# Where three blocks of attention and their output projection are woven into the rest of a hybrid attention and mLSTM layer

## The chip, the cores and the metric

One core of a Trainium2 chip runs the whole program. The metric is the device time of one execution in microseconds, the median of several runs. The engines are TensorE (PE, with its weight loads as PEld), VectorE (DVE), ScalarE (ACT), GpSimd (POOL), and SyncE (SP), whose queue issues nearly all DMAs.

## What is computed

One layer on 1152 tokens in 9 blocks of 128: block 0 is a prompt, blocks 1 to 8 are latent tokens of one request. Attention (8 query heads of 64, 2 key heads) and a bidirectional mLSTM (4 heads of 128) read one input projection, and one output projection merges them; a SwiGLU FFN of width 2816 follows. Cut to what matters:

```python
h = rmsnorm(x, norm1_w) * (1 + sc1) + sh1
aq, ak, av, mq, mk, mv, mo, mg = jnp.split(h @ w_in, SPLIT_POINTS, axis=-1)
attn_o = attention(rope(rmsnorm(aq)), keys, vals)   # prompt: own keys; latent: 1024 + 128 context keys
hm, st_f, st_b = mlstm_bidir(mq, mk, mv, gates, init_f, init_b)
hm = rmsnorm(hm, mlstm_norm_w) * sigmoid(mo)
x = x + g1 * (jnp.concatenate([attn_o, hm], axis=-1) @ w_out)
h2 = rmsnorm(x, norm2_w) * (1 + sc2) + sh2
x = x + g2 * ((silu(h2 @ w_g) * (h2 @ w_u)) @ w_down)
y = rmsnorm(x, final_norm_w)
```

All is float32; the kernel splits operands into a high and a low part and takes three products for one.

## The kernel before

The 9 blocks are treated in three groups of three (CB = 3; group c has blocks 3c to 3c + 2). The program is one long order of instructions. Work that should run side by side is written as Python generators, each `yield` a unit, and `weave(main, side, n_main, n_side)` steps `side` n_side times over n_main units of `main`, evenly. `beside` steps several generators, each at its rate; `chain` puts generators one behind another. A scheduler then orders each engine's instructions by a priority, which is the place in the program, and by when it reckons their inputs to be ready; `hot(n)` moves a block n places ahead, and `tc.issue_after(x)` has instructions on x's engine issue behind x. Each engine then runs its own order strictly.

The stages, in the order of the program:

1. Modulations, the key, value and query projections.
2. The four mLSTM heads: for each, `head_project` (its part of w_in, 96 units), woven with the scan of the head before (`head_mlstm`) and with `att`, the attention.
3. The last head's scan, with the attention's half of the output projection of group 0 (`attn_out_first`).
4. `prefill`: the mLSTM half of the output projection of all blocks, and norm2 of group 0. It steps `att` by 0.35 of a unit each of its 33 steps.
5. The FFN of group 0 (`groups`, five groups of FFN columns in GROUPS). Beside the first three (`GROUPS[:NG]`, 192 units after the first four steps) runs `attention_side`: some scales, what is left of `att`, the attention's half of the output projection of group 1, the attention of group 2, twenty empty units and the output projection of group 2. Then the attention's pools in SBUF are closed (`es_att.close()`), others open in their place, and beside the last two groups (180 units) run the features of groups 1 and 2 (`features6`).
6. The FFN of groups 1 and 2 together, with seven products in the place of eight (`pair6`, `down6`), and the end (`down_last`).

The attention of a group is the generator `attention(c, oT, done, ha, hv, spill)`. For each block it loads q (tile `qr`), transposes it on PE into a PSUM bank of tag `mm`, and copies it as a high and a low part to `qT`, of which there is one. Then for each of 8 heads: S (six products, L1128) into the one tile `S`; its maximum on DVE (L1130); exp on ACT (L1131); the scaled high part on ACT (L1134) and low part on DVE (L1135); and their transposes as DMAs of SP (L1137, L1138). After each pair of heads the values (L1152, L1153) are multiplied, one pair late. Where `spill` is given, the output of a block (`oS`) goes to DRAM (`o_d`), else it stays in three tiles `oT`. Blocks other than 0 have 1152 keys; block 0 has 128.

`attn_out` is the output projection of one group: it takes a place `home(i)` for each block's high and low part, loads a block's o from DRAM if it was spilled, loads w_out in four pieces (`out_pieces`), multiplies (L1250 to L1254) and adds to x1. A weight piece (`load_piece`) is a DMA into one of two `raw` buffers, a cast on ACT (L174) and a difference on DVE (L145). Where the o was not spilled the pieces issue behind the last transpose:

```python
with nullcontext() if spilled else tc.issue_after(loaded["turned"]):
    ws = out_pieces(0, n)
```

The working PSUM banks at that stage are four of tag `mm` (a gate and up pair takes two, a down product up to two at once, transposes one) beside three for S and one, `po`, for the values.

Of the kernel before, what the change touches and what calls it, by code (L numbers as in the profile page):

```python
# [8 lines left out]
F32 = mybir.dt.float32  # L9
F32R = mybir.dt.float32r  # L10
# [9 lines left out]
P = 128  # L20
# [5 lines left out]
NQ = 8  # L26
# [7 lines left out]
CB = 3  # L34
NCH = NB // CB
CT = CB * P
GROUPS = [(0, 4), (4, 4), (8, 4), (12, 5), (17, 5)]
# [5 lines left out]
NG = 3  # L43
# [6 lines left out]
def hybrid_step(ctx: ExitStack, tc: tile.TileContext, I: dict, O: dict):  # L50
# [11 lines left out]
    def nm(s):  # L62
        uid[0] += 1
        return f"{s}_{uid[0]}"

    def weave(main, side, n_main, n_side):

        due = 0.0
        for units in main:
            due += n_side / n_main * (units or 1)  # L70
            while due >= 1.0:
                next(side, None)
                due -= 1.0
# [5 lines left out]
    def chain(*gens):  # L79
        for g in gens:  # L80
            for v in g:
                yield v
# [20 lines left out]
    drp = ctx.enter_context(tc.tile_pool(name="drp", bufs=1, space=DRAM, reuse_waits="tile"))  # L103
# [10 lines left out]
    q_d = [drp.tile([P, 512], F32, name=f"q_d{b}") for b in range(NB)]  # L114
    hm_d = [drp.tile([P, NH, CT] if c else [CT, 512], F32, name=f"hm_d{c}") for c in range(NCH)]
    g_d = drp.tile([2, 2, D], F32, name="g_d")
    o_d = [drp.tile([P, 512], F32, name=f"o_d{i}") for i in range(CB)]
    x1_d = [drp.tile([P, D], F32, name=f"x1_d{i}") for i in range(CB)]

    ident = cp.tile([P, P], F32, name="ident")  # L120
# [868 lines left out]
    def beside(*sides):  # L989

        due = [0.0] * len(sides)
        while True:
            for i, (g, rate) in enumerate(sides):
                due[i] += rate
                while due[i] >= 1.0:
                    next(g, None)
                    due[i] -= 1.0
            yield
# [24 lines left out]
    mix_spare = [t[:, 2 * (NB + 1) * P :].rearrange("p (k x) -> p k x", k=4) for t in big]  # L1023
# [34 lines left out]
    sts = [{} for _ in range(NH)]  # L1058
# [20 lines left out]
    ap = es_att.enter_context(tc.tile_pool(name="ap", bufs=1, side="right", reuse_waits="tile"))  # L1079
    ap2 = es_att.enter_context(tc.tile_pool(name="ap2", bufs=1, side="right", reuse_waits="tile"))  # L1080
# [95 lines left out]
    def new_x1(c):  # L1176
        if c == 1:
            x1 = x1p.tile([P, CB, D], F32, name=nm("x1"))
            return [x1[:, i, :] for i in range(CB)]
        x1 = [xe.tile([P, D], F32, name=nm("x1"), tag="mx", bufs=3) for _ in range(CB)]  # L1180
        for i in range(CB):
            dma(x1[i], x1_d[i])
        return x1
# [54 lines left out]
    def row_pair(row):  # L1238
        gs = []
        for n in range(2):  # L1240
            gl = xe.tile([P, 512], F32, name=nm("hmr"), tag="hmr", bufs=2)
            dma(gl, row[n * 512 : (n + 1) * 512].rearrange("(o n) -> o n", o=1).to_broadcast([P, 512]))
            gs.append(gl)
        return gs
# [160 lines left out]
    def attn_out(a, oT, row, home, spilled=None):  # L1405

        gs = row_pair(row)
        x1, parts = a["x1"], []
        for i in range(CB):
            th, tl = home(i)  # L1410
            parts.append((th, tl))
            o = oT[i]
            if spilled:
                o = t2().rearrange("p (k x) -> p k x", k=4)
                dma(o, spilled[i].rearrange("p (k x) -> p k x", k=4))
            with hot(500):
                nc.scalar.copy(th, o)
                sub(tl, o, th.bitcast(F32), "dve")
        for n in range(2):
            with nullcontext() if spilled else tc.issue_after(loaded["turned"]):  # L1420
                ws = out_pieces(0, n)
            for i, (th, tl) in enumerate(parts):
                ps = out_block([ws], 0, th, tl)
                with hot(200):
                    add_gated(x1[i], ps, gs[n], n)
                yield
        with hot(200):
            a["rs"] = stats(x1)
        yield
# [96 lines left out]
    def six_scales():  # L1526

        dve.tensor_reduce(out=six[:, 6:7], in_=shift2[:, :, 1], axis=AX.X, op=ALU.max, apply_absolute_value=True)
        dve.tensor_reduce(out=six[:, 7:8], in_=scale2[:, :, 1], axis=AX.X, op=ALU.max, apply_absolute_value=True)
        dve.scalar_tensor_tensor(out=six[:, 7:8], in0=six[:, 7:8], scalar=float(D) ** 0.5, in1=six[:, 6:7], op0=ALU.mult, op1=ALU.add)  # L1530
        yield
        yield from power_scale(fp, ones, six[:, 7:8], six[:, 0:2])
        for t, src in ((0, scale2), (1, shift2)):
            dve.tensor_scalar(out=mods6[:, :, t], in0=src[:, :, 1], scalar1=six[:, 0:1], scalar2=None, op0=ALU.mult)
        yield
# [201 lines left out]
    done = set()  # L1737
    o1 = []
    att0 = attention(0, oT, done, 200, 100)
    att = chain(att0, attention(1, o1, set(), 200, 100, o_d))  # L1740
    weave(head_project(0, sts[0]), beside((att, 0.16),), 96, 96)
    for h in range(1, NH):
        scan = head_mlstm(h - 1, sts[h - 1])
        sts[h]["scan"] = head_mlstm(h, sts[h])
        weave(head_project(h, sts[h]), beside((scan, 0.42), (att, 0.17)), 96, 96)
        emit(scan)
    scan = sts[NH - 1]["scan"]
    first, ada, x1_first, ahead = attn_out_first(oT, done)
# [12 lines left out]
    xe = ctx.enter_context(tc.tile_pool(name="xe", bufs=1, reuse_waits="tile"))  # L1761
# [18 lines left out]
    cur, nxt = {}, {}  # L1780
# [16 lines left out]

    far = {}

    def mixing(i):  # L1800
        if i == 1:
            return mix_spare
        if i == 2:
            t = ap2.tile([P, 3 * CT], F32R, name=nm("mx"), tag="pr", bufs=2)[:, 0:1024].rearrange("p (q n) -> p q n", q=NQ)
        else:
            t = ap.tile([P, NQ, P], F32R, name=nm("mx"), tag="qT", bufs=1)
        return t[:, 0:4], t[:, 4:8]

    def mixing_mx(i):
        t = xe.tile([P, NQ, P], F32R, name=nm("mx"), tag="mx", bufs=3)  # L1810
        return t[:, 0:4], t[:, 4:8]

    def attention_side():
        yield from six_scales()
        yield from att
        yield from attn_out(nxt, o1, g_d[0, 1], mixing_mx, o_d)
        far["x1"] = new_x1(2)
        o2 = []
        yield from attention(2, o2, set())
        for _ in range(20):  # L1820
            yield
        yield from attn_out(far, o2, g_d[0, 1], mixing)

    main = groups(0, cur, GROUPS[:NG])
    with tc.issue_after(loaded["gate"]):
        for _ in range(4):
            next(main)
    side = attention_side()
    weave(main, side, 18 * sum(nf for _, nf in GROUPS[:NG]) - 24, 80)
    emit(side)  # L1830
    es_att.close()
    es_6 = ExitStack()
# [1 line left out]
    a4p = es_6.enter_context(tc.tile_pool(name="a4p", bufs=1, side="right", reuse_waits="tile"))  # L1834
    sp = es_6.enter_context(tc.tile_pool(name="sp", bufs=1, side="right", reuse_waits="tile"))
    Bt = btp.tile([P, 7, 2, 4, CT], F16, name="Bt")
    firsts = []
    feats = chain(*[features6(nxt, 1, i, Bt, firsts) for i in range(CB)], *[features6(far, 2, i, Bt, firsts) for i in range(CB)])
    main = groups(0, cur, GROUPS[NG:])
    weave(main, feats, 18 * sum(nf for _, nf in GROUPS[NG:]), 40)  # L1840
    emit(feats)
    weight_scale()
    es_f.close()
# [80 lines left out]
```

## Time and profile before

| | us |
|---|---|
| median of 3 runs | 1562.74 |
| lowest, highest | 1561.05, 1563.01 |
| profiled execution | 1565.84 |
| its span, first to last instruction | 1564.1 |

| engine | busy us | share |
|---|---|---|
| PE | 1443.9 | 92% |
| PE weight loads | 1071.6 | 69% |
| DVE | 1130.5 | 72% |
| ACT | 811.9 | 52% |
| POOL | 216.3 | 14% |

The mean granted clock of TensorE was 0.963. Times in the trace are microseconds from the span's start. L12 is line 12 of the kernel. A row of the timeline has start, length, engine, line, operation, output and inputs, number of instructions merged, and in brackets the idle time of the engine before it and what ended that. SPq and ACTq are DMA issues. Matmuls are pipelined, so a product lasts longer than the distance to the next, and a busy PE is not for that alone a full one.

### The profile page before, as it was taken

How to read it: one execution, taken by the hardware profiler on the slowest of the kernel's cores; microseconds unless marked ns; L12 is line 12 of the kernel's file. 1: busy time of each engine (PE TensorE's matmuls, PEld its weight loads, DVE VectorE, ACT ScalarE, POOL GpSimd, SP SyncE). 2: the span in 40 equal slices, each digit the busy share in tenths (PEclk: the TensorE clock that was granted, in tenths of full speed). 3: DMA queues.
4: the chain of work that ended last, by engine and by line, in shares of the span. 5: the costliest groups of instructions: out<-in, count | busy, mean ns of one | idle time of the engine just before them, and what ended most of it. 6: DMA issues, size and time to landing. Idle time of an engine off the chain costs nothing. (4 is left out here: it accounts for less than half of the span.)

```text
span 1564.1 us, 22771 instructions
## 1 busy us (share of the span) xinstructions
PE 1443.9 (92%) x8281; PEld 1071.6 (69%) x8281; DVE 1130.5 (72%) x2272; ACT 811.9 (52%) x1524; POOL 216.3 (14%) x310
## 2 busy tenths in 40 slices
PE   6889899998998899998897779989999999999994
PEld 3635567776776678888796579975666767676763
DVE  4978557676768685677776566859879596886856
ACT  4855477867666454637575366735425151523233
POOL 0121323233234243000000001010000000000000
PEclk9999999999999999999898789999999999999997
DMA  9575226563558548658585533444313030312112
GB/s 368 150 232 174 66 74 95 112 106 67 99 146 212 175 113 197 195 168 201 124 179 98 153 114 117 146 143 146 96 41 121 19 121 23 122 61 74 35 35 81
DMA packets 254454, 195.45 MB, mean 125 GB/s; under 512 B 167878, under 2 KB 209046, under 8 KB 254342
## 3 DMA queue, kind: packets, MB, share of 16 engines
q1 hardware_dynamic: 251774, 189.56, 44.9%
q10 hardware_dynamic: 2440, 4.05, 0.7%
q8 instruction: 65, 1.06, 0.3%
q14 instruction: 47, 0.39, 0.1%
q0 software_dynamic: 128, 0.39, 0.1%
HBM read 143.15 MB, written 12.47 MB: 100 GB/s over the span
## 5 line engine op out<-in xcount | busy, mean ns | idle before, releaser
L1619 PE MATMUL mm<-Bt,A 128*128 128x384 f16 x616 | 200.6, 328 | 3.4 <-ACT A L1605 3.4
L1620 PE MATMUL mm<-Bt,A 128*128 128x384 f16 x616 | 202.0, 328 | 0.0
L1621 PE MATMUL mm<-Bt,A 128*128 128x384 f16 x616 | 197.8, 327 | 0.0
L174 ACT CAST whi<-raw 128x1024 fp32r<-128x1024 f32 (+1 forms) x102 | 103.1, 1013 | 130.9 <-DMA raw<-in_w_down_dram 58.2
L145 DVE TENSOR_TENSOR wlo<-raw,whi 128x1024 fp32r<-128x1024 f32 (+1 forms) x102 | 122.5, 1203 | 54.5 <-ACT whi L174 52.3
L1135 DVE SCALAR_TENSOR_TENSOR pl<-pr,st,ph 128x1152 f16<-128x1152 f32 (+1 forms) x72 | 95.9, 1333 | 41.1 <-ACT ph L1134 39.6
L1472 PE MATMUL mm<-aTh,whi 128*128 128x384 f32 x352 | 120.7, 343 | 0.7 <-ACT whi L174 0.4
L1474 PE MATMUL mm<-aTh,wlo 128*128 128x384 f32 x352 | 120.2, 342 | 0.8 <-DVE wlo L145 0.8
L1131 ACT ACTIVATE pr<-S,st 128x1152 f32<-128x1152 f32 (+1 forms) x72 | 81.3, 1129 | 75.9 <-DVE st L1130 70.9
L1473 PE MATMUL mm<-aTl,whi 128*128 128x384 f32 x352 | 119.9, 341 | 0.0
L1128 PE MATMUL S<-kst,qT 128*128 128x384 f32 (+1 forms) x400 | 92.2, 364 | 21.7 <-ACT pr L1131 21.6
L1130 DVE TENSOR_REDUCE st<-S 128x1 f32<-128x1152 f32 (+1 forms) x72 | 88.9, 1235 | 22.5 <-PE S L1128 21.1
L525 PE MATMUL wi<-headw,hT 128*128 128x384 f16 x288 | 94.6, 328 | 0.6 <-ACT th L815 0.6
L527 PE MATMUL wi<-headw,hT 128*128 128x384 f16 x288 | 94.5, 328 | 0.0
L526 PE MATMUL wi<-headw,hT 128*128 128x384 f16 x288 | 94.5, 328 | 0.0
L1134 ACT ACTIVATE ph<-pr,st 128x1152 f16<-128x1152 f32 (+1 forms) x72 | 83.8, 1163 | 18.7 <-ACT pr L1131 5.6
L1619 PEld LDWEIGHTS <-A 128*128 128x128 f16 x616 | 60.5, 98 | 47.0 <-ACT A L1605 4.2
L1128 PEld LDWEIGHTS S<-kst,qT 128*128 128x128 f32 x400 | 73.0, 198 | 28.0 <-ACT pr L1131 25.4
L1605 ACT ACTIVATE A<-S,six 128x1024 f16<-128x1024 f32 x44 | 50.2, 1147 | 73.5 <-PE mm L1621 59.5
L1621 PEld LDWEIGHTS <-A 128*128 128x128 f16 x616 | 60.5, 98 | 40.4 <-issue 0.5
L1620 PEld LDWEIGHTS <-A 128*128 128x128 f16 x616 | 60.6, 98 | 39.5 <-issue 0.9
L1203 DVE TENSOR_TENSOR t<-mm,hmr 128x512 f32<-128x512 f32 x84 | 54.5, 685 | 39.7 <-PE mm L1689 33.3
(467 smaller groups left out, 3698.2 us busy)
## 6 DMA issues: line engine op xcount, KB each, us to landing
raw<-in_w_gu_dram SPq DMA_DIRECT2D x88, 512.0 KB, 3.5
raw<-in_w_down_dram SPq DMA_DIRECT2D x40, 512.0 KB, 4.0
a<-in_w_ada_dram SPq DMA_DIRECT2D x24, 512.0 KB, 5.5
iraw<-in_w_in_dram SPq DMA_DIRECT2D x32, 256.0 KB, 2.8
x<-in_x_sample_dram SPq DMA_DIRECT2D x11, 512.0 KB, 6.2
raw<-in_w_out_dram SPq DMA_DIRECT2D x10, 512.0 KB, 4.3
aw<-in_w_ada_dram SPq DMA_DIRECT2D x8, 512.0 KB, 5.6
aw<-in_w_ada_dram SPq DMA_DIRECT2D x16, 256.0 KB, 7.6
```

Source lines behind the costliest of these rows:

```text
L145: (dve if eng == "dve" else pool).tensor_tensor(out=out, in0=full, in1=hi, op=ALU.subtract)
L174: nc.scalar.copy(hi[:, :n], raw[:, :n])
L525: mm(ps[:, :n], ah, wh[:, k % 2, c0 : c0 + n], start=(k == 0), stop=False)
L526: mm(ps[:, :n], ah, wl[:, k % 2, c0 : c0 + n], start=False, stop=False)
L1128: mm(S[:, n, 0:w], qT[:, h, :], kst[kv][:, t, c0 + n * w : c0 + (n + 1) * w], start=(t == 0), stop=(t == 1))
L1135: dve.scalar_tensor_tensor(out=plv, in0=prv, scalar=st[:, 3:4], in1=phv, op0=ALU.mult, op1=ALU.subtract)
L1472: mm(ps, wh[:, k, :], th[:, k, :], start=(k == 0), stop=False)
L1473: mm(ps, wh[:, k, :], tl[:, k, :], start=False, stop=False)
L1474: mm(ps, wl[:, k, :], th[:, k, :], start=False, stop=(k == KD - 1))
L1619: mm(ps, wh[:, k], bt[:, 0, k], start=first and k == 0, stop=False, skip_group_check=True)
L1620: mm(ps, wh[:, k], bt[:, 1, k], start=False, stop=False, skip_group_check=True)
L1621: mm(ps, wl[:, k], bt[:, 0, k], start=False, stop=k == 3, skip_group_check=True)
```

## The change

`att` now holds the attention of all three groups. Its rate in the heads goes from 0.16 to 0.2 (the first head) and from 0.17 to 0.21 (the others). The prefill's rate is the same. The attention of group 2 is spilled to DRAM as that of group 1 is, into three more tiles, and has the default places ahead (200) as before.

In `attention_side` the order is: the scales, the output projection of group 1, then what is left of `att`. The attention of group 2, the empty units and the projection of group 2 are gone from it; it gets 39 steps over the same 192 units, where it had 80.

The projection of group 2 stands behind the closing of the attention's pools, between the features of group 1 and those of group 2, in tiles of the new pool (`a4p`, tag A4, seven buffers, which the features and later the weights use). Since its o is spilled now, its w_out pieces no longer issue behind the last transpose. That chain gets 42 steps over 180 units, where it had 40. The places of before in the attention's pools (`mix_spare` and two other tiles) are not used.

```diff
-    o_d = [drp.tile([P, 512], F32, name=f"o_d{i}") for i in range(CB)]
+    o_d = [drp.tile([P, 512], F32, name=f"o_d{i}") for i in range(2 * CB)]
...
-    att = chain(att0, attention(1, o1, set(), 200, 100, o_d))
-    weave(head_project(0, sts[0]), beside((att, 0.16),), 96, 96)
+    o2 = []
+    att = chain(att0, attention(1, o1, set(), 200, 100, o_d[0:CB]), attention(2, o2, set(), spill=o_d[CB:]))
+    weave(head_project(0, sts[0]), beside((att, 0.2),), 96, 96)
...
-        weave(head_project(h, sts[h]), beside((scan, 0.42), (att, 0.17)), 96, 96)
+        weave(head_project(h, sts[h]), beside((scan, 0.42), (att, 0.21)), 96, 96)
...
-    def mixing(i):
-        if i == 1:
-            return mix_spare
-        if i == 2:
-            t = ap2.tile([P, 3 * CT], F32R, name=nm("mx"), tag="pr", bufs=2)[:, 0:1024].rearrange("p (q n) -> p q n", q=NQ)
-        else:
-            t = ap.tile([P, NQ, P], F32R, name=nm("mx"), tag="qT", bufs=1)
-        return t[:, 0:4], t[:, 4:8]
-
-    def mixing_mx(i):
-        t = xe.tile([P, NQ, P], F32R, name=nm("mx"), tag="mx", bufs=3)
+    def mixing(tp, tag, bufs):
+        t = tp.tile([P, NQ, P], F32R, name=nm("mx"), tag=tag, bufs=bufs)
         return t[:, 0:4], t[:, 4:8]

     def attention_side():
         yield from six_scales()
+        yield from attn_out(nxt, o1, g_d[0, 1], lambda i: mixing(xe, "mx", 3), o_d[0:CB])
+        far["x1"] = new_x1(2)
         yield from att
-        yield from attn_out(nxt, o1, g_d[0, 1], mixing_mx, o_d)
-        far["x1"] = new_x1(2)
-        o2 = []
-        yield from attention(2, o2, set())
-        for _ in range(20):
-            yield
-        yield from attn_out(far, o2, g_d[0, 1], mixing)
...
-    weave(main, side, 18 * sum(nf for _, nf in GROUPS[:NG]) - 24, 80)
+    weave(main, side, 18 * sum(nf for _, nf in GROUPS[:NG]) - 24, 39)
...
-    feats = chain(*[features6(nxt, 1, i, Bt, firsts) for i in range(CB)], *[features6(far, 2, i, Bt, firsts) for i in range(CB)])
+    feats = chain(*[features6(nxt, 1, i, Bt, firsts) for i in range(CB)],
+                  attn_out(far, o2, g_d[0, 1], lambda i: mixing(a4p, "A4", 7), o_d[CB:]), *[features6(far, 2, i, Bt, firsts) for i in range(CB)])
...
-    weave(main, feats, 18 * sum(nf for _, nf in GROUPS[NG:]), 40)
+    weave(main, feats, 18 * sum(nf for _, nf in GROUPS[NG:]), 42)
```

## The prediction

> **What bounds the kernel now.** First the page: TensorE (PE) is busy in 92% of the span, so a change can only win what PE loses, 120 us in all, and the question is where that lies.
>
> ```profile
> span 1564.1 us, 22771 instructions
> PE 1443.9 (92%) x8281; PEld 1071.6 (69%) x8281; DVE 1130.5 (72%) x2272; ACT 811.9 (52%) x1524; POOL 216.3 (14%) x310
> ```
>
> Second, busy time in stretches that I cut at the stages: the four mLSTM heads (205 to 490), the FFN of blocks 0 to 2 with the rest of the attention woven in (620 to 922, in five pieces), the FFN's last two groups with the features (922 to 1040). Columns: length, then busy time and instructions of PE, PEld, DVE, ACT and POOL, then the granted clock.
>
> ```profile
> 205.00:490.00 285.00, 276.40 (x1849) 205.76 (x1847) 201.44 (x477) 209.74 (x537) 90.02 (x183) 0.99 0.56 110
> 620.00:720.00 100.00, 94.86 (x510) 83.97 (x509) 66.31 (x105) 59.91 (x90) 7.09 (x6) 1.00 0.68 194
> 720.00:765.00 45.00, 34.80 (x187) 30.64 (x186) 31.11 (x43) 27.51 (x37) 2.81 (x2) 0.85 0.73 155
> 765.00:838.00 73.00, 72.84 (x420) 65.99 (x418) 56.27 (x81) 47.15 (x68) 4.82 (x4) 1.00 0.68 148
> 838.00:885.00 47.00, 27.96 (x123) 19.47 (x122) 26.87 (x40) 21.80 (x28) 0.00 (x0) 0.75 0.59 128
> 885.00:922.00 37.00, 28.68 (x122) 23.03 (x121) 20.39 (x37) 11.18 (x16) 0.00 (x0) 0.87 0.31 95
> 922.00:1040.00 118.00, 117.67 (x637) 111.27 (x636) 85.82 (x129) 77.35 (x125) 13.86 (x10) 0.98 0.43 139
> ```
>
> I call lost what PE idles plus what the clock takes (busy time x (1 - granted clock)): 720 to 765 loses 10.2 + 5.2 = 15.4 us, 838 to 885 loses 19.0 + 7.0 = 26.0, 885 to 922 loses 8.3 + 3.7 = 12.0. Together 53.4 us in 129 us. The 73 us between them lose 0.2, 620 to 720 loses 5.1, the heads 8.6 + 2.8 = 11.4 in 285. So the stretch in which attention of blocks 6 to 8 and its output projection run is the loose one, and three waits make it up.
>
> Third, each of the three. 838 to 885, from the timeline of SP and PE (start, length) and the waits of PE (total, times, longest):
>
> ```profile
> 870.44 1.34 SPq L1138 DMA_TRANSPOSE plT<-pl  x1
> 871.83 1.11 SPq L173 DMA_DIRECT2D raw<-in_w_out_dram  x2
> 879.13 1.63 SPq L173 DMA_DIRECT2D raw<-in_w_down_dram  x2
> ...
> 838.39 0.40 PE L1216 MATMUL mm<-whi,hl 128*128 128x512 f32 x1
> 884.14 0.50 PE L1214 MATMUL mm<-whi,hl 128*128 128x512 f32 x1 [2.05 <-ACT whi L174]
> ...
> PE S L1128 <- ACT pr L1131: 8.4, 3, 2.8
> ```
>
> Between 838.4 and 884.1 PE has no FFN product. The FFN's next w_down pieces are issued at 879.1, behind the w_out pieces of the projection of blocks 6 to 8; those are told to issue after the last transpose of the attention (870.4), and there are only two raw buffers, which they get first. So the FFN starves until the attention is through, and the attention alone cannot fill PE: each S waits 2.8 us for the exp before it.
>
> 720 to 765, from the timelines of PE and ACT:
>
> ```profile
> 712.70 0.60 PE L124 MATMUL mm<-ident,qr 128*128 128x128 f32 x4
> 733.32 0.49 PE L124 MATMUL mm<-ident,qr 128*128 128x128 f32 x3
> 744.34 2.29 PE L1128 MATMUL S<-kst,qT 128*128 128x384 f32 x6 [5.57 <-ACT pr L1131]
> 757.08 0.34 PE L1472 MATMUL mm<-aTh,whi 128*128 128x384 f32 x1
> ...
> 751.75 0.58 ACT L1106 CAST qT<-mm 64x512 fp32r<-64x512 f32 x1 [0.66 <-PE S L1128]
> 755.19 0.58 ACT L1106 CAST qT<-mm 64x512 fp32r<-64x512 f32 x1
> 816.21 0.58 ACT L1106 CAST qT<-mm 64x512 fp32r<-64x512 f32 x1
> ```
>
> The q of block 7 is transposed into PSUM at 712.7 and that of block 8 at 733.3, but there is one qT, in use until block 6 has made its last S. Their banks are copied out only at 751.7 and 816.2, so from 733 to 756 two of the four working banks hold waiting q, and the FFN's next gate product (757.1) starts just after the first is freed. From 757 to 816 one bank is still held, and PE loses nothing.
>
> 885 to 922, the last one: PE and ACT again.
>
> ```profile
> 921.25 1.12 PE L124 MATMUL mm<-ident,t 128*128 128x128 f32 x4 [7.49 <-ACT t L1553]
> ...
> 916.32 1.06 ACT L1435 ACTIVATE jk<-x 128x1024 bf16<-128x1024 f32 x1 [8.62 <-DVE x L1204]
> 920.50 0.70 ACT L1553 ACTIVATE t<-x,ry 128x512 f32<-128x512 f32 x1
> ...
> 686.60 1.06 ACT L1435 ACTIVATE jk<-x 128x1024 bf16<-128x1024 f32 x1
> ```
>
> The features of blocks 3 to 5 stand in the program behind the projection of blocks 6 to 8, and ACT takes that one's sums of squares (916.3) ahead of them. Their own inputs were there with the sums of squares of 686.6.
>
> **The change, part by part.** A unit is one step of the attention's generator: 12 for the first block of three, 13 for the next, 39 for three with the last. Counted from the rates: before, the heads take 15 + 3 x 16 = 63 units, the prefill 33 steps x 0.35 = 11, and the FFN stage the other 4 and all 39 of blocks 6 to 8. After, the heads take 19 + 3 x 20 = 79, the prefill 11 again, and 27 are left: blocks 7 and 8. The heads had blocks 0 to 4 and get block 5 and the q of 6. The maxima, one for each head of a block, say that the emission is followed:
>
> ```profile
> 155.00:490.00 335.00, 45.61 (x40) 0.98 0.51 103
> 490.00:640.00 150.00, 10.82 (x8) 0.95 0.62 171
> 690.00:880.00 190.00, 32.50 (x24) 0.90 0.67 147
> ...
> 727.63 1.21 PE L1128 MATMUL S<-kst,qT 128*128 128x384 f32 x6
> 734.96 0.27 PE L1153 MATMUL po<-plT,vs 128*128 128x256 f16 x1
> 735.07 0.27 PE L1152 MATMUL po<-phT,vs 128*128 128x256 f16 x1
> ```
>
> 40 in the heads are five blocks, 8 in the prefill one, 24 after it three. A block costs PE 8 x 1.21 for S and 4 x 18 x 0.11 for the values, 17.6 us, so 16 units (1.23 blocks) are 21.7 us that leave the FFN stage and come into the heads.
>
> 1. Sixteen units more in the heads. The question is whether they find gaps or lengthen the stage.
>
> ```profile
> 205.69 0.34 PE L525 MATMUL wi<-headw,hT 128*128 128x384 f16 x1
> 205.86 0.33 PE L526 MATMUL wi<-headw,hT 128*128 128x384 f16 x1
> ...
> PE S L1128 <- ACT pr L1131: 1.1, 1, 1.1
> ```
>
> Products follow each other at 0.17 us, half of one's length, so PE is full there and the stage grows by the 21.7 us; that is paid back in the FFN stage, sum zero. What is new are stalls: DVE is at 201 and ACT at 210 of 285 us, and a denser attention competes with the heads' own chain; so far one S in this stage waited for its exp, 1.1 us. Bounds: 0, and one more time the stage's whole loss, +11. Taken +3, a quarter of that loss, since attention grows by a quarter.
>
> As the Trainium skill has it (Perfetto Trace Analysis, Identifying the Most-Contended Engine), matmul busy time tells little of headroom and the share of LDWEIGHTS time should be read. The heads' weight loads are 206 of 285 us, 72%; by that rule the added 21.7 us would fit into the heads for nothing and the forecast would be 21.7 us lower, near 1502. The rows at 205.7 speak against it, and I keep it as a rival.
>
> 2. The projection of blocks 6 to 8 moved out of the attention's side and its wait for the last transpose gone (its o now comes from DRAM, so that order isn't asked for). The FFN's pieces aren't blocked and PE has FFN work beside blocks 7 and 8. Of the 26.0 us: -26 if all is filled, -13 if the last block still ends alone for half as long. Taken -24, near the filled 765 to 838 (0.2 lost). What is late next: in the FFN stage the three blocks took 190 us, 63 each, so two need 127, and FFN work with the first projection is there for some 200: attention is done before it, if it starts by 720.
>
> 3. Half the pace there (39 units over the same 192 steps, where it was 80). The q of block 8 is then issued a block's emission, 13 units or 64 steps, after that of 7, and that of block 7 when block 6 is through; at most one bank is held, as from 757 to 816. Of the 15.4 us: -15 to 0, taken -13.
>
> 4. The features of blocks 3 to 5 directly behind the attention. Of the 12.0 us: -12 to +8 (they need memory that the attention's pools give up, and now wait for block 8 as they waited for the projection). Taken -9; their inputs are ready long before.
>
> 5. The projection beside the last two FFN groups, between the two sets of features. Its PE work is the same there. It brings four w_out loads, four casts and differences, twelve gated adds, three reloads and sums of squares into 922 to 1040, where DVE has 32 us and ACT 41 us free; what DVE and ACT did in all of 885 to 922 (20.4 and 11.2 us, the FFN's share included) fits. Bounds: 0, and the 12.0 that it lost before. Taken +3.
>
> 6. Three spills and three reloads more, on SP's queue among the transposes.
>
> ```profile
> o_d<-oS SPq DMA_DIRECT2D x3, 256.0 KB, 4.2
> ...
>   DMA t<-o_d: 5.3, 1
> ```
>
> Of the three reloads before, one was waited for, 5.3 us, because it followed its spill at once. After, twelve feature steps lie between. 0 to +5, taken +1. A spill that waits on SP holds back the transposes behind it and then the values; those have slack while the FFN fills PE.
>
> Sum: +3 - 24 - 13 - 9 + 3 + 1 = -39. The profiled execution took 1565.8 us (span 1564.1), 3.1 over the median of the runs, 1562.7; so 1526.8 for such an execution and 1524 for the median. By the ends the sum goes from -53 to +11.
>
> **Rivals.** (a) The bank stall stays: two waiting q meet again at block 7 or 8, since qT is still single. Then part 3 is 0 and part 2 perhaps -20: sum -22, 1541. For it: nothing of the buffers changes. Against: with one bank held, 59 us lost nothing. The Trainium skill (Perfetto Trace Analysis, Identifying the Most-Contended Engine) reads recurring bubbles on the engine that should be full as a shortage of buffers, which would side with this; the trace shows one such gap, not a series.
>
> (b) The features wait for the pools: transposes placed ahead of FFN products stand in PE's queue until block 8 has let go, 10 to 15 us, and the heads lose their +11: sum about -15, 1548. For it: the 7.5 us wait at 921. Against: two blocks need 127 us of 200.
>
> (c) PE is not full in the heads, as worked out in part 1: 1502.
>
> (d) Slower: in the denser heads S is queued on PE before its exp is done, as at 840 to 870. Each such wait costs 2.8 us; the heads will have 48 S's. Fourteen waits eat the 39 us, twenty give +17 and 1580. Against: one wait in 40 so far, 1.1 us.
>
> (e) Nothing: the units counted into the heads are not executed there, block 5 trails into the prefill and three blocks stay in the FFN stage, which then loses as much at its new end: 1562.
>
> **How the numbers follow.** Forecast 1524 (1509 to 1538) 0.60; (a) 0.13; (b) 0.10; (c) 0.05; (d) 0.07; (e) 0.05. For 8 in 10 the range reaches from (c) past (b): 1503 to 1550; 0.12, that is (d) and (e), is left out, and what falls beyond the bounds of a term. About 0.2% (3 us) is what a measurement of this kernel can tell from no change. Faster: 0.60 + 0.13 + 0.10 + 0.05 = 0.88; same 0.05; slower 0.07.
>
> **What would show it.** Part 1: 48 maxima by the heads' end, the stage some 22 us longer, PE idle there under 15. Part 2: FFN products on PE until the last transpose, no w_out load held behind it. Part 3: never two q transposes without their copy. Part 4: the features' first transpose without a wait of several us. Part 5: the last two groups some 17 us longer, still full. Wrong would be: S waiting for exp in the heads again and again, or a new gap of over 10 us where the pools close.

## The result and the profile after

The changed kernel took 1539.0 us (median of four runs, from 1537.7 to 1543.1; the kernel before beside it 1562.9): ratio 0.9849, 95% interval 0.9822 to 0.9875, that is 23.9 us shorter. It lies in the range of 1503 to 1550, but the forecast was 1524: somewhat over half of the 39 us came. The profiled execution took 1538.0 us; the one before stood 3 us over its median, so the two profiles differ by 27.8 us. The page after, its span and its engines:

```profile
span 1536.2 us, 22786 instructions
PE 1434.6 (93%) x8281; PEld 1071.1 (70%) x8281; DVE 1126.6 (73%) x2272; ACT 810.7 (53%) x1524; POOL 222.4 (14%) x310
```

Busy time in stretches cut at the stages (length; PE, PEld, DVE, ACT, POOL with their instructions; granted clock; DMA share; GB/s). In each kernel the four are: the heads from their first product to their last, the last head's scan, the first three FFN groups, the last two with the features. Before:

```profile
156.00:477.00 321.00, 310.27 (x2023) 225.31 (x2023) 217.00 (x530) 218.64 (x571) 100.08 (x202) 0.98 0.49 98
477.00:532.00 55.00, 46.30 (x292) 32.75 (x289) 43.60 (x124) 32.02 (x92) 26.01 (x31) 0.97 0.69 206
615.00:903.00 288.00, 253.42 (x1332) 219.17 (x1330) 192.80 (x282) 160.99 (x225) 16.46 (x14) 0.93 0.66 162
903.00:1057.00 154.00, 139.95 (x737) 129.15 (x735) 106.02 (x178) 89.32 (x144) 13.86 (x10) 0.96 0.40 131
```

After:

```profile
154.00:509.00 355.00, 334.00 (x2151) 242.51 (x2151) 243.15 (x567) 239.20 (x594) 103.45 (x199) 0.97 0.55 102
509.00:573.00 64.00, 53.30 (x327) 39.29 (x325) 49.06 (x132) 35.48 (x99) 28.08 (x35) 0.92 0.64 185
652.00:856.00 204.00, 199.98 (x1090) 182.06 (x1089) 142.07 (x207) 121.71 (x175) 17.00 (x14) 0.99 0.68 181
856.00:1028.00 172.00, 158.20 (x829) 143.42 (x827) 117.51 (x194) 99.45 (x157) 13.05 (x10) 0.98 0.47 143
```

By the prediction's own measure (lost = idle + busy x (1 - granted clock)), worked out from these rows:

| lost, us | before | after | difference |
|---|---|---|---|
| heads | 10.7 + 6.2 = 16.9 | 21.0 + 10.0 = 31.0 | +14.1 |
| last scan | 8.7 + 1.4 = 10.1 | 10.7 + 4.3 = 15.0 | +4.9 |
| FFN, three groups | 34.6 + 17.7 = 52.3 | 4.0 + 2.0 = 6.0 | -46.3 |
| FFN, two groups | 14.1 + 5.6 = 19.6 | 13.8 + 3.2 = 17.0 | -2.7 |

These make -30.0; the spans differ by 27.9, so the rest of the program gave back 2. The FFN gave 49 us, where the prediction's parts 2 to 6 had 42. The heads and the scan behind them took 19, where part 1 had 3. So 16 us more than foreseen were lost there, 7 more were won in the FFN, and 2 were given back: these are the 11 us by which the profiled execution (1538.0) missed its forecast (1526.8). By the medians the miss is 15 us, as the profiled execution before was 3 us above its median and the one after 1 us below.

The clock of a row has two places, and in the heads one in the second place is worth over 3 us. Where losses of the heads are compared below, the idle time alone (10.7 before, 21.0 after) is the firmer number.

Where the attention went, from the maxima (one for each head of a block), in the heads, the last scan, the prefill, and behind:

```profile
154.00:509.00 355.00, 53.73 (x46) 0.97 0.55 102
509.00:573.00 64.00, 2.71 (x2) 0.92 0.64 185
573.00:652.00 79.00, 10.82 (x8) 0.98 0.64 163
652.00:900.00 248.00, 21.65 (x16) 0.99 0.66 176
```

46 in the heads and 2 in the scan: block 5 got in but for two heads; two blocks were left for the FFN stage. What PE waited for in the heads of the changed kernel, from 205 on:

```profile
PE mm L1152 <- DMA phT<-ph: 5.9, 3, 3.2
PE mm L1153 <- DMA plT<-pl: 1.9, 1, 1.9
PE S L1128 <- ACT pr L1131: 1.4, 2, 0.9
```

The values wait on PE for the DMA transposes of the exp's parts, 7.8 us; before, from 205 on, neither of these two waits was there. S waits for its exp as little as before (1.4 us against 1.1). Over the whole stage, from 154 or 156, the transposes cost 9.3 us against 2.4, and S waits 4.8 us in five times against 2.8 in three.

The FFN stage. No two q wait any more (that of block 7 is copied at once; that of block 8 is transposed at 790 and waits 10 us, alone), and weight pieces are split right through the end of block 8. PE and ACT after:

```profile
728.12 0.60 PE L124 MATMUL mm<-ident,qr 128*128 128x128 f32 x4
...
728.76 0.57 ACT L1106 CAST qT<-mm 64x512 fp32r<-64x512 f32 x1
...
861.24 1.05 ACT L174 CAST whi<-raw 128x1024 fp32r<-128x1024 f32 x1 [1.99 <-DMA raw<-in_w_gu_dram]
865.92 1.31 PE L1128 MATMUL S<-kst,qT 128*128 128x384 f32 x6
872.09 0.41 PE L1472 MATMUL mm<-aTh,whi 128*128 128x384 f32 x1 [3.14 <-ACT ol L1155]
```

In the kernel before, no piece was split between the last FFN work and the projection. ACT before:

```profile
876.80 1.05 ACT L174 CAST whi<-raw 128x1024 fp32r<-128x1024 f32 x1 [7.34 <-DMA raw<-in_w_out_dram]
898.92 2.00 ACT L174 CAST whi<-raw 128x1024 fp32r<-128x1024 f32 x2 [8.52 <-PE mm L1252]
```

The second of these waits for a product of the projection (L1252). The prediction did not read that row; the experiments point to it.

### The profile page after: what moved, and what is told of

It is laid out like the page before. It is cut to its first block, busy times and chain, and to the rows that moved or that the text cites. A ratio compares the mean times of both kernels' runs of the same rounds, so it can differ in the third digit from the quotient of the medians.

```text
span 1536.2 us, 22786 instructions
## 1 busy us (share of the span) xinstructions
PE 1434.6 (93%) x8281; PEld 1071.1 (70%) x8281; DVE 1126.6 (73%) x2272; ACT 810.7 (53%) x1524; POOL 222.4 (14%) x310
## 4 chain that ended last, share of the span: by engine, by line
PE 53%; DVE 4%; DMA 4%; ACT 4%; issue 1%; POOL 1%; SPq 0%; ACTq 0%; POOLq 0%
PE mm L1621 7%; PE mm L1619 7%; PE mm L1620 7%; PE mm L1687 4%; PE mm L1688 4%; PE mm L1689 4%; PE mm L1472 3%; PE mm L1474 3%; PE mm L1473 3%; PE mm L1214 2%; PE mm L1216 2%; PE mm L1215 2%; PE mm L1250 2%; DMA raw<-in_w_gu_dram 2%; PE mm L1252 2%; PE mm L1254 1%
## 5 line engine op out<-in xcount | busy, mean ns | idle before, releaser
L1472 PE MATMUL mm<-aTh,whi 128*128 128x384 f32 x352 | 121.7, 346 | 8.8 <-ACT ol L1155 3.1
L1473 PE MATMUL mm<-aTl,whi 128*128 128x384 f32 x352 | 120.9, 343 | 0.0
L1130 DVE TENSOR_REDUCE st<-S 128x1 f32<-128x1152 f32 (+1 forms) x72 | 88.9, 1235 | 21.7 <-PE S L1128 21.2
L1128 PEld LDWEIGHTS S<-kst,qT 128*128 128x128 f32 x400 | 71.0, 194 | 10.7 <-ACT pr L1131 8.4
```

What stands on the lines that cost most here:

```text
L1128: mm(S[:, n, 0:w], qT[:, h, :], kst[kv][:, t, c0 + n * w : c0 + (n + 1) * w], start=(t == 0), stop=(t == 1))
L1472: mm(ps, wh[:, k, :], th[:, k, :], start=(k == 0), stop=False)
L1473: mm(ps, wh[:, k, :], tl[:, k, :], start=False, stop=False)
```

## The experiments

All were timed beside the kernel before on the same chip (its median there 1558.9 to 1559.6), so ratios are compared, not times across groups. The rows come from one profiled execution of each kernel. Most lie within 3 us of their median; that of the projection moved alone was 6.6 us above it, and that of the product made in place 5.0 below.

**The parts of step 2, one by one, in the kernel before.** First the wait for the last transpose alone:

```diff
-            with nullcontext() if spilled else tc.issue_after(loaded["turned"]):
+            with nullcontext():
                 ws = out_pieces(0, n)
```

> The kernel before, with only the order of the w_out pieces behind the last transpose taken away. Theory: that order starved the FFN between 838 and 885, where PE lost 26 us; without it FFN products run beside block 8, the loss there falls to 8 us or less, and the time is 1545 us (1538 to 1552). Rival: the attention's own chain, ending alone, costs that time whatever the order of the pieces is; then the gap stays and the time is 1558 to 1566.

1552.9 us, ratio 0.9957 (0.994 to 0.9973): 6 us, of a hole of 26. The stretch 838 to 885, and a row each of SP and ACT:

```profile
838.00:885.00 47.00, 31.46 (x157) 23.86 (x157) 26.70 (x42) 17.21 (x22) 0.00 (x0) 0.85 0.48 100
...
835.94 0.54 SPq L173 DMA_DIRECT2D raw<-in_w_gu_dram  x1
...
885.72 1.99 ACT L174 CAST whi<-raw 128x1024 fp32r<-128x1024 f32 x2 [2.00 <-PE mm L1252]
```

It still loses 15.5 + 4.7 = 20.3 us of 26.0, although the last w_out piece was now issued at 829.5. So the order behind the transpose was a small part. The first gate and up piece of the next FFN groups was fetched at 835.9, too, and yet no piece was split from 833 to 885.7, when a product of the projection ended the wait. The count of the FFN's products in the kernel before tells what could fill the hole; a third of the gate and up products of the stage (L1472) and of its down products (L1214), in 615 to 838 and behind (in 838 to 884 neither has any):

```profile
615.00:838.00 223.00, 65.18 (x192) 0.97 0.70 171
838.00:884.00 46.00, 0.00 (x0) 0.74 0.60 130
...
615.00:838.00 223.00, 24.20 (x60) 0.97 0.70 171
...
884.00:903.00 19.00, 4.49 (x12) 0.91 0.41 123
```

By 838 the stage's gate and up products were all done, and only 3 x 12 down products of 0.23 us were left: 8 us of work for a hole that lost 26. The rest can only be filled by the next FFN groups.

**Only the projection moved, with the spill**, rates and pace as before (with its o spilled, its pieces no longer issue behind the last transpose either, so that the edit of the run above is part of this one):

```diff
-        yield from attention(2, o2, set())
-        for _ in range(20):
-            yield
-        yield from attn_out(far, o2, g_d[0, 1], mixing)
+        yield from attention(2, o2, set(), spill=o_d[CB:])
...
     feats = chain(*[features6(nxt, 1, i, Bt, firsts) for i in range(CB)],
+                  attn_out(far, o2, g_d[0, 1], lambda i: mixing(a4p, "A4", 7), o_d[CB:]),
```

> The heads' rates and the FFN stage's pace of before; changed are only the spill of blocks 6 to 8 and the place of their projection behind the close of the pools. Theory: the gain of the change comes from here; the 26 and 12 us lost at 838 to 922 shrink to some 12 in all, the 15 us of the two waiting q stay, and the time is 1538 us (1530 to 1548). Rival: the gain comes from the attention that went into the heads; then this gives less than 10 us, 1553 or more.

1544.6 us, ratio 0.9903 (0.9882 to 0.9925): 15 us, well over half of what the whole change brings. Its two FFN stages:

```profile
611.00:845.00 234.00, 218.22 (x1184) 194.84 (x1183) 165.58 (x242) 141.10 (x200) 15.69 (x13) 0.96 0.69 178
845.00:1041.00 196.00, 173.01 (x887) 155.40 (x886) 129.19 (x212) 108.74 (x169) 13.91 (x10) 0.92 0.46 135
```

The first three groups lose 15.8 + 8.7 = 24.5 in place of 52.3, the last two 23.0 + 13.8 = 36.8 in place of 19.6: block 8 makes its last S at 882, 37 us behind the stage's end. While it does, seven pieces are split between 852 and 880, where the run above had none.

**The bank stall of 720 to 765 (step 3).** A first try had the q transposes issue behind the last S of the block before:

```diff
+                with behind("S"):
+                    for j in range(4):
+                        transpose(ps[:, j * P : (j + 1) * P], flat[:, j * P : (j + 1) * P])
```

> The kernel before, with the transposes of a block's q issued on PE behind the last S of the block ahead of it, so that a waiting q holds no PSUM bank. Theory: two banks held by waiting q made the 15 us lost between 720 and 765; the loss there falls to 4 us or less and the time is 1552 us (1546 to 1558), with some 3 us more between two blocks of attention. Rival: the FFN's products waited there for weights or ACT and the banks are a by-product; then the loss stays over 10 us and the time is 1560 to 1566.

1563.5 us, ratio 1.0023 (1.0012 to 1.0035): slower. PE, with lines one further on; L1473 is the gate product:

```profile
732.41 0.48 PE L1217 MATMUL mm<-whi,hl 128*128 128x512 f32 x1
...
751.72 0.60 PE L124 MATMUL mm<-ident,qr 128*128 128x128 f32 x4
756.58 0.53 PE L1473 MATMUL mm<-aTh,whi 128*128 128x384 f32 x1
```

From 732 to 757 there is no FFN product although no q sits in a bank until 751.7. So a late transpose is as bad as a waiting one. The reading is that the FFN's next bank is handed out behind that of the q, in the order of the program, whether the q has started or not. This run alone does not show it: the gate product also stands behind an S on PE (754.7), which waited 2.4 us for its exp. The second try gave q the bank of the values:

```diff
-                ps = bank()
+                ps = psum["po"].tile([P, 512], F32, name=nm("po"), tag="po") if "po" in psum else bank()
```

> The kernel before; from the prefill on a block's q is transposed into the bank of the values (po) in place of one of the four shared banks. Theory after the runs so far: the shared banks are handed out in the program's order, so an FFN product whose bank comes behind that of a waiting q stands still until that q is copied; with q in its own bank the loss between 720 and 765 falls from 15 to 4 us or less and the time is 11 us (6 to 15) below the kernel before. Rival: the FFN lacked weights there, or ACT's order held it; then the loss stays over 10 us and the time is within 4 us of the kernel before.

1554.5 us, ratio 0.9971 (0.9957 to 0.9984). Columns as above:

```profile
720.00:765.00 45.00, 45.00 (x253) 40.66 (x252) 35.68 (x51) 28.05 (x39) 3.62 (x3) 1.00 0.76 169
820.00:880.00 60.00, 34.23 (x145) 24.82 (x144) 35.30 (x52) 25.27 (x31) 0.00 (x0) 0.72 0.61 131
```

720 to 765 loses nothing, in place of 15.4: the shared bank was the cause of that loss. But the FFN now runs dry earlier, and 820 to 880 loses 25.8 + 9.6 = 35.4, where the kernel before loses 16.9 + 8.6 = 25.5 (43.07 busy, clock 0.80). Of 15 us, 4.5 stay.

**What holds the FFN behind the projection.** On top of that, the projection in the values' bank and without the wait:

```diff
-        ps = bank()
+        ps = psum["po"].tile([P, 512], F32, name=nm("po"), tag="po") if own else bank()
...
-            with nullcontext() if spilled else tc.issue_after(loaded["turned"]):
+            with nullcontext():
...
-                ps = out_block([ws], 0, th, tl)
+                ps = out_block([ws], 0, th, tl, a is far)
```

> As the run with q in po, and the projection of blocks 6 to 8 uses po as well, and its w_out pieces no longer issue behind the last transpose. Theory: what starved the FFN at the attention's end was the order of the shared banks (behind the projection's) and of the raw buffers together; with both gone the loss from 820 to 900 falls from 32 to 10 us or less, and the time is 29 us (20 to 36) below the kernel before. Rival: block 8's chain ending alone costs that time; then it is no more than the sum of the two single edits, some 12 to 17 us.

1556.8 us, ratio 0.9985 (0.9972 to 0.9999): nothing gained over the last. On DVE the FFN's finished products are evacuated behind the projection's:

```profile
878.38 0.69 DVE L1203 TENSOR_TENSOR t<-po,hmr 128x512 f32<-128x512 f32 x1 [1.85 <-PE po L1254]
878.98 1.28 DVE L1203 TENSOR_TENSOR t<-mm,gl 128x512 f32<-128x512 f32 x2
```

So that order was taken away too, with the projection's product by its gate made in place:

```diff
+                if a is far:
+                    dve.tensor_tensor(out=ps, in0=ps, in1=gs[n], op=ALU.mult)
+                    dve.tensor_tensor(out=x1[i][:, n * 512 : (n + 1) * 512], in0=x1[i][:, n * 512 : (n + 1) * 512], in1=ps, op=ALU.add)
+                    yield
+                    continue
```

> The kernel before with the q transposed into the bank of the values, the projection of blocks 6 to 8 in that bank too, its w_out pieces not issued behind the last transpose, and now its product with the gate made in place in PSUM, without a tile of t2 and without its place 200 ahead. Theory: what kept the FFN off PE from 826 to 882 in the run without this last part is that the evacuation of its finished down products stands behind the projection's on DVE (878.4 before 879.0). Then down products are on PE between 830 and 870, the loss of 820 to 880 falls from some 37 us to 15, and the time is 20 us shorter than that run's 1557: 1535 to 1540. Rival: the FFN also stands behind the projection in the ring of split weight pieces (a cast at 886.4 waits for a projection product): then the loss stays above 30 us and the time at 1553 to 1557.

1559.2 us, ratio 0.9993 (0.9977 to 1.0009): no gain. The loss of 820 to 880 is 32.7 us (36.94 busy of 60, clock 0.74), as the rival has it; the time is 2 us above the rival's range. DVE, PE and ACT:

```profile
825.98 1.28 DVE L1203 TENSOR_TENSOR t<-mm,gl 128x512 f32<-128x512 f32 x2
...
825.43 0.40 PE L1216 MATMUL mm<-whi,hl 128*128 128x512 f32 x1
886.11 0.44 PE L1477 MATMUL mm<-aTh,whi 128*128 128x384 f32 x1 [0.68 <-ACT whi L174]
...
884.06 2.00 ACT L174 CAST whi<-raw 128x1024 fp32r<-128x1024 f32 x2 [10.38 <-PE po L1252]
```

The evacuation now comes at once (826.0), the stage's FFN is through at 825.4, and the next group's gate product comes at 886.1, behind a cast that ends its wait with a projection product. Split pieces live in five places, one after another:

```python
piece_tags = ["wl", "ipair1", "ipair0", "wq", "iraw0"]
own = [at.tile([P, 1024], F32R, name=nm(t), tag=tag, bufs=2) for t in ("whi", "wlo")]
```

A place holds one piece, high and low. The projection's first and second w_out piece are held until its last block has been multiplied, with two w_down pieces and the third w_out piece in the other three; the fourth w_out piece and then the next group's pieces must take the places of the first two. That is a reading of the trace that fits all of these runs; a sixth place was not tried. Nor is PE's own order told apart from it: there, too, the next group's gate product stands behind the projection's products (the last before it at 884.3).

**The rates in the heads.** The rates of before, in the changed kernel, with what is left of the attention ahead of the first projection and a faster pace:

```diff
-    weave(head_project(0, sts[0]), beside((att, 0.2),), 96, 96)
+    weave(head_project(0, sts[0]), beside((att, 0.16),), 96, 96)
...
-        weave(head_project(h, sts[h]), beside((scan, 0.42), (att, 0.21)), 96, 96)
+        weave(head_project(h, sts[h]), beside((scan, 0.42), (att, 0.17)), 96, 96)
...
+        for _ in range(4):
+            next(att)
+            yield
...
-    weave(main, side, 18 * sum(nf for _, nf in GROUPS[:NG]) - 24, 39)
+    weave(main, side, 18 * sum(nf for _, nf in GROUPS[:NG]) - 24, 55)
```

> The changed kernel with the heads' rates of before (63 units in place of 79), and the 16 units put into the FFN stage at 55 steps in place of 39. Theory: the denser attention stalls the heads (PE loses 37 us there against 20 before); with the old rates the heads lose 18 to 22 us again, and the time follows how the FFN takes 54 units: 1530 to 1548 us, PE's loss moving to the place where block 8 ends, behind the close of the pools. Rival: the heads' loss has another cause than the density (the order of the program): it stays over 30 us, and the time is 1545 or more.

1556.2 us, ratio 0.9978 (0.9966 to 0.9991). Heads, and the last two FFN groups:

```profile
153.00:471.00 318.00, 309.24 (x2026) 225.75 (x2024) 217.20 (x531) 218.94 (x573) 100.80 (x203) 0.99 0.48 99
830.00:1044.00 214.00, 185.52 (x948) 164.38 (x946) 144.22 (x235) 122.26 (x185) 12.36 (x10) 0.91 0.48 137
```

The heads lose 8.8 + 3.1 = 11.9, 19 less than the changed kernel's: the density there is what costs. (The expectations speak of 37 us against 20 or 22; by the rows shown here it is 31.0 against 16.9.) But block 8 now ends 57 us behind the first three groups (last S 887, groups' end 830), and the last two lose 28.5 + 16.7 = 45.2. Halfway, with 0.18 and 0.19 in the heads and 47 steps:

> The changed kernel with rates between the two in the heads (0.18 and 0.19, 71 units) and 47 steps in the FFN stage (35 units of attention there in place of 27). Theory: the heads' loss lies between, 25 to 31 us against 37, and what is won there is lost again where block 8 ends some 30 us later, behind the close; the time is 12 to 26 us below the kernel before, not better than the changed kernel by over 3. Rival: the heads' loss is a step, at some rate, and not a slope; then it is near 18 or near 37.

1554.6 us, ratio 0.9974 (0.996 to 0.9989): the heads lose 16.7 (317.51 busy of 331, clock 0.99), the last two groups 37.3 (167.41 of 193, clock 0.93); block 8's last S is at 883, the groups end at 851. The 12 to 26 us of the expectation did not come. The heads lose as much as with 63 units before (16.9), by the idle time alone 13.5 against 10.7, so most of the rise lies between 71 and 79 units; three rates do not tell a step from a slope that steepens.

**The features twelve steps later** in the changed kernel (twelve empty units ahead of them, 56 steps for 42):

> The changed kernel with twelve empty steps ahead of the features of blocks 3 to 5 and 64 steps in place of 42, so that they are placed in the program about when block 8 is through (885 us). Theory: the features' transposes, placed at 857, held banks until block 8 let go of the pools; without that the 10 us lost between 855 and 905 fall to 3 or less and the time is 8 us (3 to 12) below the changed kernel, 29 to 36 below the kernel before. Rival: ACT, with exp, casts and sums at once, is what was late there; then nothing changes and it is 20 to 27 below the kernel before.

1536.7 us, ratio 0.9846 (0.9823 to 0.9869), as the changed kernel.

```profile
856.00:903.00 47.00, 46.28 (x287) 44.81 (x286) 31.75 (x47) 36.49 (x59) 4.21 (x4) 1.00 0.64 172
854.00:1030.00 176.00, 159.63 (x836) 143.53 (x834) 123.13 (x202) 101.64 (x159) 14.16 (x10) 0.98 0.48 142
```

What the changed kernel loses at 856 to 903 (6.9 + 1.6 = 8.5) is gone, and the stage as a whole still loses 16.4 + 3.2 = 19.6: the waits come later.

**A faster pace** in the changed kernel, 56 steps for 39:

> The changed kernel with 56 steps of the attention's side over the same 192 units, where it had 39, so that it is written out after two thirds of the stage. Theory: what the changed kernel still loses at 856 to 903 (some 9 us) comes from block 8 ending 12 us after its place in the program; ended by 850 it goes: 1530 to 1533. Rival: at that pace the q of block 8 waits in a bank again and the FFN stands behind it, as in the kernel before (up to 15 us), or the attention alone isn't faster: 1539 to 1552.

1542.4 us, ratio 0.9897 (0.988 to 0.9914). Block 8's last S starts at 864 in place of 866, the first three groups end at 863, and lose 11.1 + 6.1 = 17.3, in place of 6.0:

```profile
647.00:863.00 216.00, 204.87 (x1090) 185.53 (x1090) 145.02 (x210) 125.23 (x178) 16.24 (x13) 0.97 0.65 174
```

The q of block 8 was transposed at 758 and copied at 798. Writing the attention out earlier doesn't make it faster, only the q wait longer.

**Eight units moved from the heads to the prefill** (0.18 and 0.19 in the heads, 0.6 for 0.35 in the prefill):

```diff
-        due += 0.35
+        due += 0.6
```

> The changed kernel with 0.18 and 0.19 of a unit in the heads (71 units, where 0.2 and 0.21 gave 79) and 0.6 in the prefill (20 units, where 0.35 gave 11), so that the FFN stage has 26 units, as the changed kernel's 27. Theory: the loss in the heads comes from the density of attention there (37 us at 79 units, 22 at 71), and the prefill, at 97% PE, takes eight units at less: 5 to 10 us gained, 1529 to 1534. Rival: the prefill pays as much as the heads win, or block 5 and 6 trail so that block 8 ends late: 1539 to 1555.

1530.4 us, ratio 0.9819 (0.9802 to 0.9837): the lowest of all, and within its expectation. Its interval overlaps that of the changed kernel (0.9822 to 0.9875), which was run beside another series of the kernel before, so the step between them is not clear of noise by the times; what follows compares one trace with one trace. Heads, last scan, prefill, and the two FFN stages:

```profile
153.00:485.00 332.00, 318.73 (x2078) 232.68 (x2078) 225.09 (x542) 228.07 (x580) 93.96 (x200) 0.98 0.53 101
485.00:546.00 61.00, 50.92 (x325) 37.84 (x323) 51.88 (x135) 37.88 (x98) 26.58 (x34) 0.97 0.72 202
546.00:633.00 87.00, 79.94 (x426) 65.69 (x427) 72.44 (x160) 49.42 (x79) 34.97 (x27) 0.98 0.65 159
633.00:844.00 211.00, 203.21 (x1109) 183.80 (x1109) 143.78 (x214) 126.06 (x181) 18.19 (x14) 0.99 0.68 183
844.00:1018.00 174.00, 160.95 (x834) 146.03 (x832) 119.53 (x197) 100.46 (x158) 17.93 (x10) 0.96 0.46 141
```

The heads lose 13.3 + 6.4 = 19.6 (31.0 in the changed kernel) and the scan 10.1 + 1.5 = 11.6 (15.0); the prefill, which was not at 97% but at 92% PE in the changed kernel, takes its share at 8.7 (7.9: 72.59 busy of 79, clock 0.98), and the FFN stages lose 9.8 and 19.5 (6.0 and 17.0). Sum -7.7, the span 1527.0 in place of 1536.2. The same with 50 steps in the FFN stage:

> As the one with more attention in the prefill and less in the heads, and with 50 steps of the attention's side where that has 39, so that its end is written out after 77% of the stage. If both theories hold (density in the heads, lateness of block 8), 1525 to 1530; if the attention trails out of the heads by as much as it starts later, the faster pace pulls it back and this one is 5 to 15 us faster than the one with 39; if waiting q cost more, it is slower than that one.

1535.8 us, ratio 0.9852 (0.9831 to 0.9873), by the medians 5 us slower than with 39, though the intervals just overlap. Block 8's last S starts at 851 in place of 855, and a q waits from 749 to 785. The first three groups:

```profile
633.00:861.00 228.00, 210.91 (x1139) 188.26 (x1138) 152.28 (x225) 132.51 (x188) 18.24 (x14) 0.99 0.67 174
```

That is 17.1 + 2.1 = 19.2 lost, in place of 9.8. That the waiting q makes the difference is read from the trace; it was not tried by itself.

## Why the prediction was right, and where it was not

The direction, the place of the gain and the range held; the forecast itself was 15 us too low. Two of its working steps are wrong as they stand. By the ends of its terms the sum goes up to +23, not +11 (the 12 of part 5 are left out). And not each S waits 2.8 us at 838 to 885: three of five do. Neither enters the forecast. Step by step:

1. **Sixteen units more in the heads, taken +3: measured +14 in the heads and +5 in the scan behind.** This is the term that was mis-sized, and it came above its upper bound (11). That the added products lengthen the stage was right. The step that failed is "a quarter of that loss, since attention grows by a quarter": loss doesn't grow in proportion. With 63 units the heads lose 11.9 to 16.9 us, with 71 15.9 to 19.6, with 79 27.5 (330.11 busy of 351, clock 0.98, at the faster pace) to 31.0. By the idle time alone it is 8.8 to 10.7, 12.8 to 13.5, and 20.9 to 21.0. What is shown is that the loss follows the density (three rates, and back again); that it comes through the transposes of the exp's parts is read from the waits (over the whole stage 7 us more of them, of 10 us more idle time) and wasn't tried by itself.

2. **Projection moved, taken -24, and 3. half the pace, taken -13.** The first three groups lost 46 us less, which also holds some of the 12 us of step 4, as that stretch ends at 903. For step 3 the cause stands: 720 to 765 loses 0.8 after (44.18 busy of 45), no two q wait, and another bank for q alone clears it. For step 2 the size was about right in the whole change and the cause was wrong in the main. The order behind the transpose, with the raw buffers, is a small part: without it 6 us came. By 838 that stage had 8 us of FFN work left, and the next groups stood behind the projection, by the reading above in the ring of split pieces. With the projection behind the close they don't; that move alone gave 15 us, where steps 2, 4, 5 and 6 together had 29; the attention of three blocks then ended 37 us behind the stage. The prediction saw that w_down pieces came late and took the first delay in the row for the whole of it. That the size came out all the same is luck: by this reading the move also took the projection out of a second queue, which the prediction had not read.

   "Two blocks need 127 us, attention is done before the stage's end if it starts by 720" failed. Block 7's first S came at 734, the two took 150 us with their values, and the last values ended at 884, 28 us behind the first three groups. It cost 8.5 us, since FFN work of the next groups was there.

4. **Features directly behind the attention, taken -9, and 5. the projection in the last two groups, +3.** These two groups became 18 us longer (17 foreseen), and lose 17.0 in place of 19.6. No feature waits 7.5 us; the longest wait of one is 2.2 us.

6. **Spills, +1.** No wait of PE for a spill or reload appears among the waits from 856 on.

The rivals. (a), the bank stall, did not come at 39 steps; at 50 and 56 one q waited for 35 to 40 us, and the stage lost 19.2 and 17.3. (What the Trainium skill says of recurring bubbles, on which (a) draws, stands in Perfetto Trace Analysis under Optimization Strategy, and says only that they can mean such a shortage.) (b) came in small, the 8.5 us at 856 to 903; later features moved that loss and didn't end it. (c) fell: the heads grew by 34 us. By the Trainium skill (Perfetto Trace Analysis, Identifying the Most-Contended Engine) the headroom of TensorE is judged by the share of weight loads, beside the operations done as a share of the peak. The share of weight loads was 70% in the heads before and 68% after (225 of 321, 243 of 355), and no room was there; the other measure was not worked out. (d) fell by its own mechanism (S waited five times in the whole stage, 4.8 us in all), but its place was right: the dense heads cost most. (e) was seen in a trace only: two of block 5's maxima trail into the scan.

Taken over the runs, the loss at the end goes with how far the attention ends behind the first three FFN groups. Start of block 8's last S less the groups' end, and what the last two groups lose: -10 us and 15.8 (prefill with 50 steps), 1 and 16.1 (faster pace), 10 and 17.0 (changed kernel), 11 and 19.5 (prefill), 12 and 19.6 (later features), 32 and 37.3 (halfway), 37 and 36.8 (projection alone moved), 57 and 45.2 (heads back). So the heads' share is not free to give back either: it has to go to a stage that can take it. Which of the resources behind the close waits for block 8 there was not settled.

## What to carry to other kernels

When an engine starves beside a late piece of work, count how much of its own stage's work is left, and ask in what order every shared place (PSUM banks, raw and split weight buffers, the other engines' queues) is handed out: here taking away one to three of them gave 0 to 6 us, and moving the late work behind the others' place in the program gave 15. The price of side work in a full stage can rise faster than the amount, as it did here between 71 and 79 units; spread it over the stages and measure two rates before the sum is believed. A side chain that is written out earlier isn't done earlier when it is bound by itself; it only holds its buffers longer.

## What the runs showed of the hardware

A hole can cost more than its idle time. In the run with the product in place, 826 to 873 has PE busy for 25.8 of 47 us at a granted clock of 0.67, so 8.5 us on top of 21.2 idle, and its gate products take 0.53 us at 890.9 and 0.34 at 892.8. And the issue of a DMA transpose, 1.3 us as a rule, can take several times that in the denser heads; just ahead of two of the waits for transposes (2.1 us at 280.8 and 1.9 at 282.9) SP's queue in the changed kernel has

```profile
269.51 1.28 SPq L1137 DMA_TRANSPOSE phT<-ph  x1
270.96 6.76 SPq L1138 DMA_TRANSPOSE plT<-pl  x1
```

At the same place it took 6.13 us at the faster pace, and at the heads' end (476.0) another took 9.29; in the kernel before, the longest in the heads from 205 on took 2.6 us. What held them wasn't tried.
